# Two PSUM copies on ScalarE and eight token differences on GpSimd in a hybrid convolution and RWKV-7 step

## The chip, the cores and the metric

The kernel runs on one core of a Trainium2 chip. A core has a matrix engine (TensorE, PE in the profile, with its weight loads as PEld), a vector engine (VectorE, DVE), a scalar engine (ScalarE, ACT), a general engine (GpSimd, POOL), a queue engine that only issues transfers (SyncE, SP), and DMA engines. Each engine works through its own queue of instructions in order, and semaphores hold an instruction until what it needs is there. The metric is the device time of one execution in microseconds; 2640.5 us is the median of three runs before the change (2638.36 to 2641.32).

## What is computed

One inference step of a two-layer decoder over 1040 prompt positions (16 learned ones and 1024 tokens) and 8 separate single tokens. Layer 0 is a Conformer convolution and an MLP, layer 1 is an RWKV-7 time mixing and an MLP. The change concerns layer 1's mixer:

```python
def _wkv7_step(S, inp):
    r_t, w_t, k_t, v_t, kk_t, a_t = inp
    sa = jnp.einsum('bhvk,bhk->bhv', S, -kk_t)
    S = (S * w_t[:, :, None, :] + sa[..., None] * (kk_t * a_t)[:, :, None, :]
         + v_t[..., None] * k_t[:, :, None, :])
    y = jnp.einsum('bhvk,bhk->bhv', S, r_t)
    return S, y

def _rwkv7(h, shift_prev, S0, x_mix, w_r, w_k, w_v, w_o, ...):
    prev = jnp.concatenate([shift_prev[:, None, :].astype(h.dtype), h[:, :-1]], axis=1)
    xx = prev - h
    xr = h + xx * x_mix[0]
    ...
    r = (xr @ w_r).astype(f32)
    ...
    S_final, ys = lax.scan(_wkv7_step, S0.astype(f32), xs)
    ...
```

`xx` is the difference of each token's normalised row from the row before it. Every projection of the mixer reads a mixture `h + xx * x_mix[i]`. The scan updates one 64 x 64 state for each of 16 heads.

## The kernel before

Feature rows are kept transposed: 1024 features lie as KT = 8 blocks of 128 partitions, tokens run along the free dimension. Layer 0 goes through the tokens in three groups (352, 348, 348), the mixer in four (272, 256, 256, 264), layer 1's output projection and MLP again in three. The MLPs split each operand into a rounded high part and a remainder: for every weight tile, ScalarE writes the high part (`load_w`, L158) and GpSimd the remainder in four subtractions of 256 columns (L165), and TensorE multiplies three times (L190 to L192). Five buffers hold the split weight tiles.

The mixer's differences are made in `prepare`. It loads `hx` (the normalised rows with the row before the group), and then for each of the eight blocks makes `xx` at L893, by GpSimd for blocks 2 and 5 and by VectorE for the other six. The mixture `mix` (L887, tile mx) reads `xx`. For the first group `prepare(0)` is called while layer 0's MLP still works on its last token group; each difference is placed with `issue_after` behind a remainder `hl` (L142) of that MLP, block k behind the remainder number k + 5. In that MLP, VectorE also rescales (L347) and adds the products to the residual h (L360), which frees the PSUM banks that TensorE's `out` products fill.

The recurrence runs in 17 chunks of 64 tokens (the first holds the 16 learned positions). Each chunk turns the scan into small matrix products over 16 heads. `front(c)` forms A (L1287) and moves its parts to SBUF by ScalarE (no, L1292) and VectorE (xa, L1295; nr, L1297). `chunk(c)` then forms gg, the transposes bT (L1356), W (L1363), copied by VectorE as w1 (L1365), po, and U (L1379), which is a triangular solve applied to W. U fills one PSUM bank: 128 partitions by 8 blocks by 64. Partitions 0 to 63 hold the first head of each pair and 64 to 127 the second. L1380 copies the lower half by VectorE into `uv[HALF[0], :, 0, :]`, L1381 the upper half by ScalarE into `uv[HALF[1], :, 1, :]`. The state product S (L1390) and the output product Y (L1399) read `uv`. fs and sv (L1405, L1408) on VectorE make the next state.

The banks for A, W, U, S, Y, and the transposes yn (L1559) of finished chunks, come from one PSUM pool of three ("w"); a tile that asks for a bank waits until the readers of its last owner are done.

The chunks are woven into the projections: generators yield waits, and `tick` and `advance` decide after which projection a chunk's next step is emitted. TensorE's order is that of the program (`manual_schedule` for the tensor engine around the mixer and layer 1's MLP). The queues of VectorE, ScalarE and GpSimd are written there by a planner that simulates the program with estimated durations; instructions marked `kept_place` hold their place in the program's order. So on these three engines the order of instructions is a result of the planner's estimates.

Of the kernel before, what the change touches and what calls it, by code (L numbers as in the profile page):

```python
# [43 lines left out]
HALF = [slice(0, HS), slice(HS, P)]  # L44


def hybrid_step(tc, x_prompt, x_sample, state_conv, state_shift, state_wkv, meta_tokens,
# [8 lines left out]
    nc = tc.nc  # L56
    ctx = ExitStack()
    with ctx:
# [57 lines left out]
        def vec(name, i):  # L116
            c = col[name] + i
            return pvec[:, c:c + 1]
# [75 lines left out]
        def bank(name, tag="mm"):  # L194
            return cur[tag].tile([P, 512], F32, name=name, tag=tag)
# [672 lines left out]
        def prepare(g):  # L868

            c0, n = G1[g]  # L870
            npr = min(c0 + n, NP_TOK) - c0
            nm = lambda s, *a: f"{s}{g}" + "".join(f"_{x}" for x in a)

            hx = hnp.tile([P, KT, 1 + N1], F32, name=nm("hx"), tag="hx")
            if g == 0:
                nc.gpsimd.memset(hx[:, :, 0:1], 0.0)
                nc.sync.dma_start(hx[:, :, 1:1 + n], d_hn[:, :, :n])
            else:
                nc.sync.dma_start(hx[:, :, :1 + n], d_hn[:, :, c0 - 1:c0 + n])
            yield  # L880
            xx = hnp.tile([P, KT, N1], F32, name=nm("xx"), tag="xx")

            def mix(i, k):

                t = mixp.tile([P, N1], F32, name=nm("mx", i, k), tag="mx")
                with nullcontext() if g else tc.issue_after(marks["out2"][2 * (k - KT) + 1 if i == 2 else -1]):
                    nc.vector.scalar_tensor_tensor(t[:, :n], xx[:, k, :n], vec("x_mix", i * KT + k), hx[:, k, 1:1 + n],  # L887
                                                   op0=ALU.mult, op1=ALU.add)
                return t[:, :n]
            act = []  # L890
            for k in range(KT):
                with tc.issue_after(decayed[g - 1] if g else marks["hl2"][k + 5]):
                    (nc.gpsimd if k % 3 == 2 else nc.vector).tensor_sub(xx[:, k, :npr], hx[:, k, 0:npr], hx[:, k, 1:1 + npr])  # L893
                    if npr < n:
                        nc.vector.tensor_sub(xx[:, k, npr:n], sps[:, k], hx[:, k, 1 + npr:1 + n])
                if g:
                    act.append(mix(2, k))
                yield
            prep[g] = mix, hx, act
# [67 lines left out]
        def mixer_in(g, tick):  # L967
# [148 lines left out]
            for p in range(KT):  # L1116
# [81 lines left out]
                if g < 3:  # L1198
                    if p == 0:
                        coming = ranked(PP, prepare(g + 1))  # L1200
                        next(coming)
                    if p == 1:
                        for _ in coming:
                            pass
                        ks = carry["keys"] = keys(g + 1, both)
                        next(ks)
                    for _ in keys_behind(p):
                        next(ks, None)
# [53 lines left out]
        kv = lambda t: t.rearrange("p (k v) -> p k v", k=KT)  # L1262
# [60 lines left out]
        def chunk(c):  # L1323
# [3 lines left out]
            sv, uv = st["sv"], st["uv"]  # L1327
# [6 lines left out]
            def quads(name, pairs, lhs, rhs):  # L1334
                ps = bank(f"{name}{c}", "w")
                for p in range(KT):
                    for i, o in pairs:
                        nc.tensor.matmul(ps[Q[o], p * 32:(p + 1) * 32], lhs(i, p), rhs(i, p), start=True, stop=True,
                                         tile_position=(32 * i, 32 * o))
                return ps, ps[:, :256].rearrange("p (k t) -> p k t", k=KT)  # L1340
            down, up = [(0, 1), (2, 3)], [(1, 0), (3, 2)]

            ps, _ = quads("gg", down, lambda i, p: no[Q[i], p, :], lambda i, p: x32[Q[i], p, :])
# [9 lines left out]
            for h in range(2):  # L1353
                ps = bank(f"bT{c}{h}", "w")
# [5 lines left out]
            ps = bank(f"W{c}", "w")  # L1360
# [15 lines left out]
            ps = bank(f"U{c}", "w")  # L1376
            for p in range(KT):
                for q in range(2):
                    nc.tensor.matmul(ps[HALF[q], p * HS:(p + 1) * HS], p64[HALF[q], p, :], w1[HALF[q], p, :], start=True, stop=True)  # L1379
            nc.vector.tensor_copy(uv[HALF[0], :, 0, :], kv(ps)[HALF[0]])  # L1380
            nc.scalar.copy(uv[HALF[1], :, 1, :], kv(ps)[HALF[1]])  # L1381
            yield RW[5]
            step(c + 1)
            yield RW[6]
# [2 lines left out]
            ps = bank(f"S{c}", "w")  # L1387
# [39 lines left out]
        def recurrence():  # L1427
            for c in range(NCH):
                yield from chunk(c)
# [174 lines left out]
        with in_order():  # L1604
            shift_in()
            for _ in prepare(0):
                pass
            carry["keys"] = keys(0, lambda: None)
            for _ in range(KT + 1):
                next(carry["keys"])  # L1610
            for g in range(4):
                mixer_in(g, lambda slow=1.0: tick(g, slow))
            for _ in range(4):
                tick(3, 1.0)
            carry["tail"]()
            invert()
            settle(-(-(sum(G2[0]) - META) // HS))
# [183 lines left out]
```

## Time and profile before

| | |
|---|---|
| median of three runs | 2640.5 us (2638.36 to 2641.32) |
| profiled execution | 2641.17 us, its span 2639.5 us |
| instructions | 51709 |
| mean granted TensorE clock | 0.993 |
| DMA | 400.24 MB, mean 152 GB/s |

The profile gives a busy time for each engine, the chain of work that ended last, groups of instructions by source line with mean duration and the idle time before them, and who waited for whom. A timeline row reads: start in us, us, engine, line, operation, output<-inputs, shapes, count, and in brackets the idle time of the engine before it with what ended that. A row with a count above one merges neighbours, and its time is that of all of them. A row of the view of stretches reads: from:to, length, the busy time of PE, PEld, DVE, ACT and POOL with their counts, the granted clock of TensorE, the DMA engines' share and GB/s. Layer 0 takes the time up to some 1060 us, the mixer from there to about 1705 us, with the last chunks of the recurrence woven into layer 1's output projection and MLP up to 1902 us.

### The profile page before, as it was taken

The page shows a single profiled execution, that of the slowest core. Times are in us where ns is not written, and L with a number is a line of the kernel's source. Part 1 is how long each engine was busy: PE and PEld are TensorE (multiplying, and loading weights), DVE is VectorE, ACT ScalarE, POOL GpSimd, SP SyncE. Part 2 cuts the span into 40 slices and gives each one's busy share as a digit, 9 for nine tenths or more (in the row PEclk, how much of TensorE's full clock was granted, in tenths as well). Part 3 has the DMA queues.
Part 4 walks back from the last instruction along what each step waited for, and adds up shares of the span by engine and source line. Part 5 has one row for each costly group of instructions (what it writes and reads, how often), then busy time and mean ns, then how long its engine had stood idle before and what let it go on. Part 6 is the DMA issues. An engine that isn't in the chain of part 4 may idle for free.

```text
span 2639.5 us, 51709 instructions
## 1 busy us (share of the span) xinstructions
PE 2584.5 (98%) x19956; PEld 2439.1 (92%) x19956; DVE 1720.5 (65%) x3610; ACT 1129.0 (43%) x2093; POOL 1453.0 (55%) x2060
## 2 busy tenths in 40 slices
PE   9999999999999999999999999999999999999998
PEld 8999999999999999877787877799999999999998
DVE  6999999997544444544867567686689544444435
ACT  5546435444534333233344545555444542222223
POOL 7677878878878777122111213476588763333331
PEclk9999999999999999999999999999999999999999
DMA  6663544554446543678876867898575542222211
GB/s 189 174 164 111 163 142 132 161 171 137 142 137 179 157 137 119 181 202 205 227 191 191 217 170 189 217 206 195 149 215 174 147 132 68 69 72 64 73 49 45
DMA packets 602060, 400.24 MB, mean 152 GB/s; under 512 B 96128, under 2 KB 548928, under 8 KB 601814
## 3 DMA queue, kind: packets, MB, share of 16 engines
q1 hardware_dynamic: 573764, 360.08, 49.7%
q0 software_dynamic: 8720, 26.35, 3.2%
q10 hardware_dynamic: 19330, 10.49, 1.4%
q8 instruction: 158, 2.59, 0.4%
q14 instruction: 88, 0.72, 0.1%
HBM read 338.94 MB, written 58.83 MB: 151 GB/s over the span
## 4 chain that ended last, share of the span: by engine, by line
PE 86%; DVE 8%; DMA 2%; ACT 2%; issue 1%; POOL 0%; ACTq 0%; SPq 0%; DVEq 0%; POOLq 0%
PE ps_in L190 8%; PE ps_in L192 8%; PE ps_in L191 8%; PE out L190 8%; PE out L191 8%; PE out L192 8%; PE pk L922 4%; PE pr L922 4%; PE pv L922 3%; PE ps_g L190 1%; PE ps_o L192 1%; PE ps_g L191 1%; PE ps_g L192 1%; PE ps_oo L190 1%; PE ps_o L190 1%
## 5 line engine op out<-in xcount | busy, mean ns | idle before, releaser
L165 POOL TENSOR_TENSOR wo_lo<-wo_raw,wo_hi 128x256 fp32r<-128x256 f32 x736 | 541.9, 769 | 286.2 <-ACT wo_hi L158 282.4
L165 POOL TENSOR_TENSOR wi_lo<-wi_raw,wi_hi 128x256 fp32r<-128x256 f32 x640 | 473.5, 772 | 241.7 <-ACT wi_hi L158 241.1
L190 PE MATMUL out<-hh,wo_hi 128*128 128x352 f32 (+2 forms) x1536 | 497.6, 324 | 10.5 <-DVE h L360 8.9
L360 DVE TENSOR_TENSOR h<-h,out 128x352 f32<-128x352 f32 (+2 forms) x768 | 386.7, 512 | 167.1 <-PE out L192 165.7
L190 PE MATMUL ps_in<-m_h,wi_hi 128*128 128x352 f32 (+2 forms) x1536 | 493.9, 322 | 0.0
L192 PE MATMUL ps_in<-m_l,wi_hi 128*128 128x352 f32 (+2 forms) x1536 | 492.7, 321 | 0.7 <-DVE m_l L288 0.7
L191 PE MATMUL out<-hh,wo_lo 128*128 128x352 f32 (+2 forms) x1536 | 492.5, 321 | 0.0
L191 PE MATMUL ps_in<-m_h,wi_lo 128*128 128x352 f32 (+2 forms) x1536 | 491.5, 320 | 0.0
L192 PE MATMUL out<-hl,wo_hi 128*128 128x352 f32 (+2 forms) x1536 | 490.8, 320 | 0.0
L542 DVE SCALAR_TENSOR_TENSOR cv<-u,wdw,cv 128x348 f32<-128x348 f32 (+2 forms) x720 | 378.9, 578 | 0.7
L158 ACT CAST wi_hi<-wi_raw 128x1024 fp32r<-128x1024 f32 x160 | 167.6, 1048 | 386.9 <-PE out L192 194.6
L158 ACT CAST wo_hi<-wo_raw 128x1024 fp32r<-128x1024 f32 x184 | 192.6, 1048 | 313.0 <-PE out L192 166.6
L190 PEld LDWEIGHTS out<-hh,wo_hi 128*128 128x128 f32 x1536 | 289.1, 188 | 16.4 <-DVE h L360 11.7
L190 PEld LDWEIGHTS ps_in<-m_h,wi_hi 128*128 128x128 f32 x1536 | 289.2, 188 | 1.5
L192 PEld LDWEIGHTS ps_in<-m_l,wi_hi 128*128 128x128 f32 x1536 | 288.2, 188 | 2.0 <-DVE m_l L288 1.5
L191 PEld LDWEIGHTS out<-hh,wo_lo 128*128 128x128 f32 x1536 | 288.5, 188 | 0.8
L191 PEld LDWEIGHTS ps_in<-m_h,wi_lo 128*128 128x128 f32 x1536 | 288.5, 188 | 0.6
L192 PEld LDWEIGHTS out<-hl,wo_hi 128*128 128x128 f32 x1536 | 288.2, 188 | 0.0
L347 DVE SCALAR_TENSOR_TENSOR ps_in<-ps_in,rs_m 128x352 f32<-128x352 f32 (+2 forms) x192 | 100.6, 525 | 256.1 <-PE ps_in L192 255.7
L142 DVE TENSOR_TENSOR hl<-ps_in,hh 128x352 fp32r<-128x352 f32 (+2 forms) x192 | 98.9, 515 | 124.0 <-ACT hh L141 123.9
L348 ACT ACTIVATE ps_in<-ps_in 128x352 f32<-128x352 f32 (+2 forms) x192 | 85.1, 444 | 129.5 <-DVE ps_in L347 129.3
L1099 POOL DMA_DIRECT2D d_n<-n x32 | 24.4, 762 | 189.1 <-DVE n L1089 97.6
(371 smaller groups left out, 4735.1 us busy)
## 6 DMA issues: line engine op xcount, KB each, us to landing
wi_raw<-in_w_mlp_in_dram SPq DMA_DIRECT2D x160, 512.0 KB
wo_raw<-in_w_mlp_out_dram SPq DMA_DIRECT2D x160, 512.0 KB
wk_raw<-in_rwkv_w_k_dram SPq DMA_DIRECT2D x32, 512.0 KB
wr_raw<-in_rwkv_w_r_dram SPq DMA_DIRECT2D x32, 512.0 KB
wv_raw<-in_rwkv_w_v_dram SPq DMA_DIRECT2D x32, 512.0 KB
d_ab<-ab POOLq DMA_DIRECT2D x32, 512.0 KB, 4.5
pg_raw<-in_conv_w_pw_dram SPq DMA_DIRECT2D x24, 512.0 KB
pa_raw<-in_conv_w_pw_dram SPq DMA_DIRECT2D x24, 512.0 KB
```

The source lines that it names most:

```text
L142: return eng_lo.tensor_sub(lo, src, hi.bitcast(F32))
L158: cast = nc.scalar.copy(hi[:, :a * b], raw[:, :a * b])
L165: eng_lo.tensor_sub(lo[:, cs], raw[:, cs], hi[:, cs].bitcast(F32))
L190: nc.tensor.matmul(ps, w[0], act[0], start=first, stop=False)
L191: nc.tensor.matmul(ps, w[1], act[0], start=False, stop=False)
L192: nc.tensor.matmul(ps, w[0], act[1], start=False, stop=last)
L347: nc.vector.scalar_tensor_tensor(s, s, 0.0, rs()[:, :n], op0=ALU.max, op1=ALU.mult)
L348: nc.scalar.activation(s, s, AF.Square)
L360: total = nc.vector.tensor_add(hv[:, 4 * i + m, :], hv[:, 4 * i + m, :], ps[:, :n])
L542: nc.vector.scalar_tensor_tensor(acc[m][:, :n], ug[:, m, j:j + n], wdw[:, m, j:j + 1], acc[m][:, :n], op0=ALU.mult, op1=ALU.add)
L922: nc.tensor.matmul(ps[:, :n], w[:, k, :], act[k], start=k == 0, stop=k == KT - 1)
L1099: nc.gpsimd.dma_start(d_n[ch0:ch0 + ncg, p].rearrange("c r t -> r c t"), n32[:, :ncg])
```

## The change

Two edits. In `prepare`, all eight differences of the first group go to GpSimd; the other three groups stay as they were. In `chunk`, both halves of U are copied by ScalarE, one after the other, in all 17 chunks.

```diff
                 with tc.issue_after(decayed[g - 1] if g else marks["hl2"][k + 5]):
-                    (nc.gpsimd if k % 3 == 2 else nc.vector).tensor_sub(xx[:, k, :npr], hx[:, k, 0:npr], hx[:, k, 1:1 + npr])
+                    (nc.gpsimd if k % 3 == 2 or not g else nc.vector).tensor_sub(xx[:, k, :npr], hx[:, k, 0:npr], hx[:, k, 1:1 + npr])
...
             for p in range(KT):
                 for q in range(2):
                     nc.tensor.matmul(ps[HALF[q], p * HS:(p + 1) * HS], p64[HALF[q], p, :], w1[HALF[q], p, :], start=True, stop=True)
-            nc.vector.tensor_copy(uv[HALF[0], :, 0, :], kv(ps)[HALF[0]])
-            nc.scalar.copy(uv[HALF[1], :, 1, :], kv(ps)[HALF[1]])
+            for q in range(2):
+                nc.scalar.copy(uv[HALF[q], :, q, :], kv(ps)[HALF[q]])
             yield RW[5]
```

## The prediction

> **What bounds the kernel now.** The first view is the page: the engines' shares and the chain of work that ended last.
>
> ```profile
> PE 2584.5 (98%) x19956; PEld 2439.1 (92%) x19956; DVE 1720.5 (65%) x3610; ACT 1129.0 (43%) x2093; POOL 1453.0 (55%) x2060
> ...
> PE 86%; DVE 8%; DMA 2%; ACT 2%; issue 1%; POOL 0%; ACTq 0%; SPq 0%; DVEq 0%; POOLq 0%
> ```
>
> TensorE (PE) sets the end, and the change touches none of its instructions. So the question is narrow: which of TensorE's waits does the change shorten or create? The second view is the list of who TensorE waited for (total us, times, longest).
>
> ```profile
> PE out L190 <- DVE h L360: 8.9, 8, 2.3
> PE bT L1356 <- DVE nr L1297: 4.5, 5, 3.3
> PE A L1287 <- DVE fs L1405: 3.6, 2, 2.6
> PE yn L1559 <- ACT uv L1381: 3.2, 1, 3.2
> PE gg L1338 <- ACT em L1159: 3.0, 1, 3.0
> PE Y L1397 <- DVE nr L1297: 2.6, 2, 1.6
> ```
>
> Two single waits stand out: the longest on h (2.3) and the one on uv (3.2). The change edits the neighbourhood of both. GpSimd (POOL) ends none of the long ones.
>
> **Part one: token differences of the first group.** The tile view of xx (ns, minimum/median/maximum; the mixing mx in the whole run, the differences up to 1060 us), then the timelines of the three engines:
>
> ```profile
> L887 DVE SCALAR_TENSOR_TENSOR mx<-xx,pvec,hx x128: 460/485/1291, 1062.9 to 1546.7; 128x256 f32<-128x256 f32 x64, 128x272 f32<-128x272 f32 x32, 128x264 f32<-128x264 f32 x32
> L893 DVE TENSOR_TENSOR xx<-hx x6: 434/505/5217, 863.1 to 921.8; 128x272 f32<-128x272 f32 x6
> L893 POOL TENSOR_TENSOR xx<-hx x2: 642/642/643, 855.6 to 856.2; 128x272 f32<-128x272 f32 x2
> 855.62 1.24 POOL L893 TENSOR_TENSOR xx<-hx 128x272 f32<-128x272 f32 x2 [3.29 <-DMA hx<-d_hn]
> 856.82 5.62 POOL L165 TENSOR_TENSOR wi_lo<-wi_raw,wi_hi 128x256 fp32r<-128x256 f32 x8
> 862.39 5.59 POOL L165 TENSOR_TENSOR wo_lo<-wo_raw,wo_hi 128x256 fp32r<-128x256 f32 x8
> 871.19 1.43 POOL L165 TENSOR_TENSOR wi_lo<-wi_raw,wi_hi 128x256 fp32r<-128x256 f32 x2 [3.21 <-ACT wi_hi L158]
> 863.06 5.22 DVE L893 TENSOR_TENSOR xx<-hx 128x272 f32<-128x272 f32 x1
> 868.20 0.93 DVE L360 TENSOR_TENSOR h<-h,out 128x348 f32<-128x348 f32 x2
> 868.76 0.43 PE L190 MATMUL out<-hh,wo_hi 128*128 128x348 f32 x1 [2.33 <-DVE h L360]
> ```
>
> One difference on VectorE (DVE) took 5.22 us where the shortest took 0.434. It began while GpSimd ran sixteen subtractions without a pause (856.82 to 862.39 + 5.59 = 867.98) and finished 0.3 us after them. Behind it stood the additions L360 that empty PSUM, and TensorE stood 2.33 us for them. The change takes all six differences away from VectorE, so nothing of this kind is left there. Gain: at most 2.33, since no wait gives back more than its length; at least 0, if another late link ends at the same place. I take 2.33, because the additions have no other work of VectorE ahead of them.
>
> What it adds: six differences on GpSimd, 6 x 0.642 = 3.85 us. If all stand where the two stand now, GpSimd's stream reaches its 871.19 work about 3.85 - 3.21 = 0.64 us late. What hides it: the first weight tile behind the differences is done halfway through the eight subtractions at 856.82, near 859.6, and TensorE first uses it at the row below, 10.3 us later. Without that cover it would be 3.85 us; with it, I count nothing.
>
> ```profile
> 869.98 0.32 PE L191 MATMUL ps_in<-m_h,wi_lo 128*128 128x348 f32 x1
> ```
>
> Queued behind the moved differences are only these weight tiles; no DMA moves. The wait for hx (3.29) stands at the head already. The mixing mx that reads xx starts at 1062.9, far from the last difference at 921.8.
>
> **Part two: the U copies, once in each of 17 chunks.** The tile view of U, with the waits that ended at its readers:
>
> ```profile
> L1380 DVE COPY uv<-U x17: 657/682/684, 1306.9 to 1897.1; 64x512 f32<-64x512 f32 x17
> L1381 ACT COPY uv<-U x17: 581/582/585, 1307.6 to 1897.8; 64x512 f32<-64x512 f32 x17
>   DVE uv L1380: 32.5, 14
>   PE U L1379: 5.4, 9
> ```
>
> The two halves do not run side by side today: ScalarE (ACT) stood 32.5 us in 14 chunks until VectorE's half was done. So two copies on ScalarE replace a chain of 0.682 + 0.582 = 1.26 by 2 x 0.582 = 1.16, with no handover and no place in VectorE's queue. ScalarE's busy time grows by 17 x 0.582 = 9.9 us, while 32.5 us of standing still go. The place where this reaches TensorE is chunk 3:
>
> ```profile
> 1436.14 1.15 PE L1379 MATMUL U<-w,p 64*64 64x64 f32 x32
> 1434.78 1.51 ACT L1535 ACTIVATE ez<-yn,pvec 128x128 f32<-128x128 f32 x4 [0.46 <-ACT vt L1072]
> 1441.74 0.68 DVE L1380 COPY uv<-U 64x512 f32<-64x512 f32 x1
> 1442.46 0.58 ACT L1381 COPY uv<-U 64x512 f32<-64x512 f32 x1 [6.17 <-DVE uv L1380]
> 1438.76 1.16 PE L1287 MATMUL A<-xa,bk 64*128 64x128 f32 x16
> 1443.09 0.66 PE L1559 MATMUL yn<-ident,ey 128*128 128x128 f32 x4 [3.17 <-ACT uv L1381]
> ```
>
> U ends at 1437.29 and ScalarE is free from 1436.29, but VectorE reaches its half at 1441.74. The transposes yn need the PSUM bank that U occupies, so TensorE stands 3.17 us. With both copies on ScalarE the bank is free at about 1437.3 + 1.2 = 1438.5, before A ends at 1439.92. Gain: between 0 and 3.17; I take 3.17. Late next are the PSUM readers of A on VectorE, whose queue gets 0.6 us shorter.
>
> Taking 0.68 from VectorE also shortens its queue elsewhere. That counts only where its work is unbroken from the copy to something TensorE waits for.
>
> ```profile
> 1569.60:1583.50 13.90, 9.79 (x169) 8.26 (x165) 13.32 (x37) 4.95 (x15) 3.00 (x6) 0.92 0.49 115
> 1599.50:1604.00 4.50, 3.61 (x50) 2.81 (x48) 4.45 (x13) 1.09 (x3) 1.97 (x5) 1.00 0.35 102
> 1599.50 0.68 DVE L1380 COPY uv<-U 64x512 f32<-64x512 f32 x1
> 1600.11 0.34 DVE L1350 TENSOR_SCALAR p<-p,par32q 128x256 f32<-128x256 f32 x1
> 1604.05 0.65 PE L1397 MATMUL Y<-sv,xa 128*64 128x64 f32 x15 [0.94 <-DVE nr L1297]
> 1583.54 0.69 PE L1356 MATMUL bT<-ident,bk 128*128 128x128 f32 x2 [3.31 <-DVE nr L1297]
> ```
>
> In the stretch rows (length, busy us of PE, PEld, DVE, ACT and POOL, then the granted clock) VectorE is busy 13.32 of 13.90 and 4.45 of 4.50, each from a copy to a wait on nr. The next instruction starts 1600.11 - 1599.50 = 0.61 later, so about 0.6 comes off each: 1.2 us. Bounds: 0, and 17 x 0.61 = 10.4 if every chunk passed it on.
>
> The cost: ScalarE's second copy delays what stands behind it, by up to 0.58, where ScalarE comes late by itself.
>
> ```profile
> 1570.49 0.58 ACT L1381 COPY uv<-U 64x512 f32<-64x512 f32 x1
> 1573.43 0.39 PE L1390 MATMUL S<-uv,bkt 128*64 128x64 f32 x5
> ```
>
> There the pair would end near 1571.65 and S reads it at 1573.43; the cover is 1.8 us. I count nothing; without cover it is at most 0.58 a chunk, 9.9 us over all 17.
>
> **The sum.** The profiled execution took 2641.17 us, its span being 2639.5. Minus 2.33, 3.17 and 1.2 gives 2634.5. The median of the three runs shown, 2640.5, lies 0.7 below that execution, so I forecast 2634. What the sum cannot price is order: the queues of ScalarE, VectorE and GpSimd are arranged by a planner from estimated times, and both parts change these times, so other instructions may swap places. The clock makes such a swap dearer than its wait:
>
> ```profile
> 1615.50 0.70 PE L1338 MATMUL gg<-x,no 32*32 32x32 f32 x19 [3.04 <-ACT em L1159]
> 1615.30:1622.10 6.80, 6.49 (x49) 5.48 (x50) 4.15 (x15) 2.56 (x8) 1.06 (x4) 0.50 0.51 116
> 1436.20:1444.60 8.40, 5.22 (x64) 4.36 (x64) 8.37 (x22) 1.19 (x4) 2.15 (x4) 1.00 0.26 75
> ```
>
> After the 3.04 us wait, TensorE ran 6.8 us at clock 0.50; half of its 6.49 busy us, 3.25, was lost on top: 6.3 in all. After the 3.17 us wait of chunk 3 the clock stayed at 1.00, so I count only that wait's own length. A swap is worth -6.3 to +6.3 by this row; I take 0 and keep both ends.
>
> The Trainium skill ("TensorE: Matmul & The Clock Gate", section "What's actually happening") says that the gate watches a free-running window of 4096 cycles, 3413 ns, and halves the clock after an idle one. The 6.8 us stretch is two such windows; that a wait slightly longer than 3.04 left the clock alone fits a window that does not start with the wait.
>
> **The rivals.** *Slower: ScalarE becomes late.* In the recurrence, ScalarE's tanh, exp and vv feed the scan and TensorE; it stood ahead of TensorE's waits on em (3.0, in the list). If the planner puts the pair of copies in front of such work, ScalarE stands at U with it behind. Two such places, in a kernel that keeps only part one: 2640.5 - 2.3 + 2 x 6.3 = 2651. It decides from 7.6 us of new waits, beyond one such place. For it: the planned order can move anywhere between 1300 and 1900 us. Against it: ScalarE already stands 32.5 us at these copies, and would wait there for U alone.
>
> *Part two passes on.* TensorE gets past yn and stops soon after at other work of VectorE, which is booked solid there: 8.37 of 8.40 us. Then part one remains: 2640.5 - 2.3 = 2638. Against it: the yn group needs nothing else of VectorE.
>
> *Relief throughout.* If nearly every chunk passes on 0.61: 2640.5 - 2.3 - 3.2 - 10.4 = 2625. Against it: waits on nr and fs together are 10.7 us in the list, at few places.
>
> *The clock.* Work that comes 2.3 to 5.5 us earlier meets the gate's windows elsewhere. One stretch of 6.8 us fewer or more is about 3.3: 2631 or 2637. The clock row above bears out that waits of equal length differ; which way it falls is open.
>
> *The change does not do what it says*: the eight differences are spread over later gaps of GpSimd. The gain is the same, since VectorE is clear of them either way; no separate time.
>
> **How the numbers follow.** Chances: forecast 0.36 (own range 2629 to 2638), ScalarE late 0.25, part two passed on 0.16, relief throughout 0.12, the clock 0.11. About 0.2%, 5.3 us, is what a measurement can tell from no change: faster means below 2635.2, slower above 2645.8. Faster: 0.28 of the forecast, 0.11 of the relief, 0.06 of the clock, 0.45. Slower: 0.24 of ScalarE late. The rest, 0.31, is the same. The range from 2623 to 2651 reaches the relief and half of the slower case.
>
> **What would show it.** Right: eight xx on GpSimd before 930 us, at about 0.64 each and none on VectorE; no 2.3 us wait of TensorE near 866; 34 uv copies on ScalarE at 0.58, waiting for U alone; no wait of yn near 1437; VectorE busy some 19 us less (17 x 0.68, and the six differences with the held one). Wrong: a new wait of TensorE on GpSimd's weight tiles near 870, on em, vv or no of ScalarE between 1300 and 1900, or more stretches at clock 0.50 than before.

## The result and the profile after

| | before | after |
|---|---|---|
| median, us | 2641.3 | 2637.85 |
| ratio of the times, 95% interval | | 0.9984 [0.9978, 0.9990] |
| profiled execution, its span, us | 2641.17, 2639.5 | 2637.09, 2635.4 |
| granted clock of that execution | 0.993 | 0.994 |

The changed kernel is 0.16% faster, 4.2 us. The median came out 3.9 us above the 2634 that was forecast. Two of the 22 executions after the change took 3618.78 and 6682.36 us; the median counts them, the ratio and all means of spans below leave them out. First the engines' shares after the change and, of the list of who TensorE waited for (total us, times, longest), the rows that bear on the change:

```profile
PE 2581.3 (98%) x19956; PEld 2436.7 (92%) x19956; DVE 1707.6 (65%) x3587; ACT 1139.1 (43%) x2110; POOL 1457.0 (55%) x2066
...
PE out L190 <- DVE h L360: 7.6, 7, 1.6
PE A L1287 <- DVE fs L1405: 4.4, 4, 2.4
PE bT L1356 <- DVE nr L1297: 4.3, 4, 3.3
PE Y L1397 <- DVE nr L1297: 3.6, 2, 2.0
PE gg L1338 <- DVE ni L1250: 2.3, 1, 2.3
PE ps_oo L192 <- DVE z_l L142: 1.3, 1, 1.3
```

The wait on uv is gone from the list, and so is the 2.3 us wait on h. In their place stand two more waits on fs, a longer sum on nr at Y, a longer wait on z_l (0.4 before), and a shorter one at gg. TensorE's 19,956 matmuls are in the same order as before, so the two traces can be laid side by side matmul by matmul. The tile views of xx and uv, and the timeline around chunk 3's U, then its later row on fs:

```profile
L893 POOL TENSOR_TENSOR xx<-hx x8: 641/642/650, 855.1 to 862.0; 128x272 f32<-128x272 f32 x8
L1381 ACT COPY uv<-U x34: 572/581/585, 1301.9 to 1892.6; 64x512 f32<-64x512 f32 x34
  PE U L1379: 12.7, 11
...
1432.76 1.15 PE L1379 MATMUL U<-w,p 64*64 64x64 f32 x32
1433.95 1.17 ACT L1381 COPY uv<-U 64x512 f32<-64x512 f32 x2 [1.06 <-PE U L1379]
1435.37 1.16 PE L1287 MATMUL A<-xa,bk 64*128 64x128 f32 x16
1436.46 0.66 PE L1559 MATMUL yn<-ident,ey 128*128 128x128 f32 x4
1449.76 0.67 DVE L1405 TENSOR_TENSOR fs<-S,wc 128x512 f32<-128x512 f32 x1
1450.48 1.16 PE L1287 MATMUL A<-xa,bk 64*128 64x128 f32 x14 [0.66 <-DVE fs L1405]
```

The row of before at the same place on fs has no wait:

```profile
1455.96 1.16 PE L1287 MATMUL A<-xa,bk 64*128 64x128 f32 x16
```

The change does what it says. ScalarE's pair begins 0.04 us after U ends (1433.91), is done at 1435.12, and yn follows A without a wait. But 14 us later TensorE, which no longer stood for VectorE at yn, stands 0.66 us at fs, which it did not do before. Aligned by index, from start to start, the traces show 3.25 us won at yn (the lead goes from 3.38 to 6.63 us) and 1.14 us of it lost at fs and in A behind it (to 5.49).

### The profile page after: what moved, and what is told of

Same layout as the page of the kernel before. It is cut to its first block, busy times and chain, and to the rows that moved or that the text cites. A ratio compares the mean times of both kernels' runs of the same rounds, so it can differ in the third digit from the quotient of the medians.

```text
span 2635.4 us, 51726 instructions
## 1 busy us (share of the span) xinstructions
PE 2581.3 (98%) x19956; PEld 2436.7 (92%) x19956; DVE 1707.6 (65%) x3587; ACT 1139.1 (43%) x2110; POOL 1457.0 (55%) x2066
## 4 chain that ended last, share of the span: by engine, by line
PE 84%; DVE 9%; DMA 2%; ACT 2%; issue 2%; POOL 1%; ACTq 0%; SPq 0%; DVEq 0%; POOLq 0%
PE ps_in L190 8%; PE ps_in L192 8%; PE ps_in L191 8%; PE out L190 8%; PE out L191 8%; PE out L192 8%; PE pk L922 4%; PE pr L922 4%; PE pv L922 3%; PE ps_o L192 1%; PE ps_o L190 1%; PE ps_o L191 1%; PE ps_g L190 1%; PE ps_g L191 1%; PE ps_g L192 1%
## 5 line engine op out<-in xcount | busy, mean ns | idle before, releaser
L190 PEld LDWEIGHTS out<-hh,wo_hi 128*128 128x128 f32 x1536 | 289.1, 188 | 15.0 <-DVE h L360 10.4
```

What stands on the lines that cost most here:

```text
L190: nc.tensor.matmul(ps, w[0], act[0], start=first, stop=False)
```

## The experiments

Every ratio is against the kernel before, timed beside it on the same chip. "Clock" is the granted clock of a run, averaged over the runs of a kernel; the kernel before has 0.9929 over 101 runs. A mean clock of 11 or 12 runs is uncertain by about 0.0006 either way (twice its standard error), that of c3c7 by 0.0011.

| kernel | ratio, 95% interval | mean span, us | clock |
|---|---|---|---|
| part one alone (p1_only) | 1.0003 [0.9995, 1.0012] | 2640.9 | 0.9929 |
| block 0's difference alone (k0_only) | 0.9999 [0.9991, 1.0008] | 2640.1 | 0.9927 |
| first group all on VectorE (first_dve) | 1.0006 [0.9997, 1.0015] | 2640.7 | 0.9926 |
| the kernel before, again (before_again) | 1.0003 [0.9995, 1.0012] | 2640.3 | 0.9928 |
| part two alone (p2_only) | 0.9983 [0.9974, 0.9993] | 2635.5 | 0.9947 |
| part two in chunk 3 alone (c3_only) | 0.9991 [0.9982, 1.0000] | 2636.8 | 0.9932 |
| part one, and chunk 3 (c3_p1) | 0.9992 [0.9983, 1.0001] | 2638.4 | 0.9928 |
| part two but chunk 3 (but_c3) | 1.0000 [0.9991, 1.0009] | 2640.0 | 0.9937 |
| part two in chunks 3 and 7 (c3c7) | 0.9991 [0.9982, 1.0001] | 2637.6 | 0.9935 |
| part two but chunk 7 (p2_but_c7) | 0.9987 [0.9978, 0.9996] | 2636.7 | 0.9940 |
| part two but chunk 5 (p2_but_c5) | 0.9981 [0.9973, 0.9990] | 2635.0 | 0.9945 |
| the kernel after, again (after_again) | 0.9984 [0.9975, 0.9993] | 2635.7 | 0.9948 |

### Which part carries it

Part one alone, then part two alone:

```diff
-                    (nc.gpsimd if k % 3 == 2 else nc.vector).tensor_sub(xx[:, k, :npr], hx[:, k, 0:npr], hx[:, k, 1:1 + npr])
+                    (nc.gpsimd if k % 3 == 2 or not g else nc.vector).tensor_sub(xx[:, k, :npr], hx[:, k, 0:npr], hx[:, k, 1:1 + npr])
```

> Only the first edit: all eight differences of the first group on GpSimd, the U copies as before. The instruction order of ScalarE and SyncE stays as before, TensorE's too. My theory (one difference on VectorE was held 4.8 us by GpSimd's unbroken stream, and TensorE stood 2.33 us behind it): TensorE's wait of 2.33 near 866 us is gone, every later instruction of TensorE comes 2.4 us earlier, and the whole is 2.4 us shorter: ratio 0.9991. Rival (the clock's windows decide): the waits of the recurrence meet the windows elsewhere and the end moves by 2.4 plus or minus 3.3 us. Rival (GpSimd pays): a new wait on a weight tile near 870, and the ratio is 1.000.

```diff
-            nc.vector.tensor_copy(uv[HALF[0], :, 0, :], kv(ps)[HALF[0]])
-            nc.scalar.copy(uv[HALF[1], :, 1, :], kv(ps)[HALF[1]])
+            for q in range(2):
+                nc.scalar.copy(uv[HALF[q], :, q, :], kv(ps)[HALF[q]])
```

> Only the second edit: both halves of U copied by ScalarE in all 17 chunks. My theory (TensorE gains 3.0 us in chunk 3, and swapped instructions of the queues and waits for VectorE take back about 1.5 to 2.5 by the end): 0.5 to 2 us shorter, ratio 0.9992 to 0.9998. Rival (the two parts are independent and the second is worth what is left of 4.1 after 2.4): 1.7 us shorter with the same waits at the chunk 5 and 7 outputs (2.0 and 1.6 us) as with both edits. Rival (the copies themselves cost ScalarE's users): longer than before, ratio above 1.000.

Part two alone has the whole gain; part one has none. Yet part one's trace seemed to confirm the forecast: at 868 us it wins 2.6 us, counted from start to start, on the first profile of before (its lead goes from 0.62 to 3.22 us). Moving only block 0's difference shows the same 2.6 us, and no gain either:

```diff
+                    (nc.gpsimd if k % 3 == 2 or g + k == 0 else nc.vector).tensor_sub(xx[:, k, :npr], hx[:, k, 0:npr], hx[:, k, 1:1 + npr])
```

> Of the first group's differences only block 0 moves from VectorE to GpSimd, which then has blocks 0, 2 and 5; VectorE keeps 1, 3, 4, 6 and 7. No other instruction changes its place. My theory (only the difference that meets GpSimd's unbroken stream is held; the others fall where GpSimd pauses): the whole gain of the first edit, 2.4 us, ratio 0.9991, and the five differences left on VectorE at 0.43 to 0.51 us. Rival (the next difference on VectorE meets the longer stream in its place): one of the five takes 2 us or more, TensorE waits again, and less than 1 us is gained.

That left a lead that was won and never arrived. Two kernels went after it: one with all eight differences of the first group on VectorE, and the kernel before itself.

```diff
+                    (nc.gpsimd if k % 3 == 2 and g else nc.vector).tensor_sub(xx[:, k, :npr], hx[:, k, 0:npr], hx[:, k, 1:1 + npr])
```

> Neither part; instead all eight xx of the first group stand on VectorE, so that GpSimd begins its unbroken stream after nothing of the group. My theory (the 5.22 us of block 0 is time in which GpSimd's back-to-back operations hold VectorE's two-source operation): the stream begins earlier, at hx's arrival less nothing, and VectorE's first xx is held again as long as that stream lies in its way, so a held xx of 3 to 6 us appears again on VectorE and TensorE's wait near 866 us stays at 2 us or more. Rival (it was GpSimd's own two differences that delayed it): all eight run at about 0.38 us each, the wait near 866 is under 0.5 us and the trace is 2.3 us ahead there. By the end of the trace either is worth under 1 us, ratio 0.9996 to 1.0005, as with part one alone.

> The kernel before itself, unchanged, profiled a second time. My theory: every wait of TensorE over 0.5 us comes back with the same place and length to 0.1 us, while the stretches at clock 0.50 move, because they start at other multiples of the same step; so the two traces drift apart by 1 to 4 us at those stretches and nowhere else, and the ratio is 1.0000 within 0.0008. Rival (the clock stretches belong to the program): the same stretches at the same places to 1 us, and the traces agree to 0.5 us all along; then what part one lost at 1440 us is the change's own doing.

The timelines of the second profile of before, around the place where the first one has the 5.22 us difference:

```profile
856.10 5.64 POOL L165 TENSOR_TENSOR wi_lo<-wi_raw,wi_hi 128x256 fp32r<-128x256 f32 x8
861.68 5.84 POOL L165 TENSOR_TENSOR wo_lo<-wo_raw,wo_hi 128x256 fp32r<-128x256 f32 x8
862.86 0.57 DVE L893 TENSOR_TENSOR xx<-hx 128x272 f32<-128x272 f32 x1
863.35 1.54 DVE L360 TENSOR_TENSOR h<-h,out 128x348 f32<-128x348 f32 x3
866.07 0.32 PE L190 MATMUL out<-hh,wo_hi 128*128 128x348 f32 x1
1441.47 0.66 PE L1559 MATMUL yn<-ident,ey 128*128 128x128 f32 x4 [3.17 <-ACT uv L1381]
```

The same program, with the same unbroken run of sixteen subtractions on GpSimd, took 0.57 us for the difference, and TensorE went on at 866.07 without a wait. The wait on yn came back to the hundredth. So the 5.22 us belongs to one execution and the 3.17 us to the program. Nine profiles have block 0's difference on VectorE. It took 5.22 us in the first one of before and 0.43 to 1.03 us in the other eight (with all eight differences on VectorE, 0.43 us, GpSimd's run has pauses there), and all eight win the same 2.6 us on that first profile at this place, with part one or without. My theory of part one falls: what it removes is an event that came once in nine profiles. The rival expectation for the kernel with all eight on VectorE (no wait, some 2.3 us ahead) came true, but not by its reason, since the unchanged kernel does the same.

The second profile of before also shows where leads go. It was 3.1 us ahead of the first at 1266 us and ended 2.4 us behind it. Part of this is at a decode step woven into layer 1. The rows of the first profile, then of the second:

```profile
1933.04 0.43 DVE L1485 TENSOR_TENSOR t<-Sdec,dq 128x256 f32<-128x256 f32 x1 [1.99 <-DMA dq<-d_dec]
1934.87 0.63 DVE L1487 TENSOR_TENSOR Sdec<-Sdec,dq 128x256 f32<-128x256 f32 x1
1937.98 0.43 PE L190 MATMUL out<-hh,wo_hi 128*128 128x328 f32 x1 [1.13 <-DVE h L360]
```

```profile
1932.42 1.01 DVE L1485 TENSOR_TENSOR t<-Sdec,dq 128x256 f32<-128x256 f32 x1 [2.06 <-DMA dq<-d_dec]
1934.82 0.86 DVE L1487 TENSOR_TENSOR Sdec<-Sdec,dq 128x256 f32<-128x256 f32 x1
1938.15 0.60 PE L190 MATMUL out<-hh,wo_hi 128*128 128x328 f32 x1 [1.99 <-DVE h L360]
...
1938.20:1941.60 3.40, 3.40 (x13) 3.40 (x14) 2.61 (x7) 1.05 (x1) 0.35 (x2) 0.50 0.50 74
```

VectorE began 0.62 us earlier, but two of its operations took 0.81 us more, and TensorE, 0.69 us ahead, waited 0.86 us longer; a half-clock stretch followed, which the first profile does not have there. My expectation that TensorE's long waits come back to 0.1 us, with the drift at the clock alone, was thus wrong: those at yn, Y, gg, bT and U do, those on vv, fs (2.60 and 4.16 us near 1715) and h move by up to 1.6 us.

### Chunk 3 and the other sixteen chunks

Part two in chunk 3 alone, first with part one and then without it, and after them in every chunk except 3:

```diff
-            nc.vector.tensor_copy(uv[HALF[0], :, 0, :], kv(ps)[HALF[0]])
+            (nc.scalar.copy if c == 3 else nc.vector.tensor_copy)(uv[HALF[0], :, 0, :], kv(ps)[HALF[0]])
```

> The first edit, and the second in chunk 3 alone; the other 16 chunks copy as before. ScalarE's order differs by the one copy only, VectorE's by a few neighbours. My theory (the gain sits in two places, and what was lost came from swapped neighbours in the queues of chunks 5 and 7): both waits gone, 2.4 + 3.0 us, less 0.9 where TensorE meets VectorE in chunk 4: 4.5 us shorter, ratio 0.9983, and the waits of TensorE for nr in chunks 5 and 7 stay at 1.6 and 0.9. Rival (TensorE being earlier by itself brings the waits, since VectorE sets the pace there): these waits grow as with the full change, to 2.0 and 1.6, and the whole is 2.5 us shorter. Rival (the relief of VectorE in the other 16 chunks carries the gain): hardly shorter than the first edit alone.

> Part two in chunk 3 alone, the difference on VectorE as before. My theory: the yn wait of 3.17 us near 1437 us goes, some 0.9 of it returns as a wait on fs near 1456, and nothing else of part two happens, so -2.2 us, ratio 0.9991; the vv wait at 1266 and the nr waits of chunks 5 and 7 stay as before. Rival (the gain of part two is ScalarE's and VectorE's new order in all chunks): chunk 3 alone is worth under 1 us, ratio over 0.9996. Rival (clock windows set the time): the yn wait goes and the end still lies within 1 us of before, because a stretch at clock 0.50 stands somewhere where before has none.

```diff
+            (nc.scalar.copy if c != 3 else nc.vector.tensor_copy)(uv[HALF[0], :, 0, :], kv(ps)[HALF[0]])
```

> Part two in every chunk except 3, the difference as before. My theory: the yn wait of chunk 3 stays at 3.2 us, the vv wait of 0.67 at 1266 goes, the nr waits of chunks 5 and 7 grow by 0.4 and 0.7: together +0.4 us, ratio 1.0002, so that chunk 3 is all of part two. Rival (relief of VectorE in the other sixteen chunks is worth as much as chunk 3): -2 us, ratio 0.9992, with smaller waits on fs, no or h after 1700 us. The two ratios, this one and that of chunk 3 alone, must add up to that of part two alone (-0.0017) if the chunks act independently.

In the traces these behave as expected: with chunk 3 the yn wait goes and 0.65 to 0.87 us comes at fs; without it yn keeps 3.16 us. By ratio chunk 3 is worth 0.0009 and 0.0008, close to its net 2.1 us in the traces, the rest 0.0000, and part two whole 0.0017. With intervals of 0.0009 to either side, a remainder of 0.0008 is no proof that the parts need each other. But one column of the table separates better than the times: the granted clock. It is 0.9926 to 0.9932 in the kernels without part two or with chunk 3 alone, and 0.9945 to 0.9948 in part two alone, without chunk 5, and in the changed kernel in both its measurements. What that is worth is read within one kernel; the table has the three values that both kernels have:

| granted clock of the run | before: runs, mean span us | after, both measurements: runs, mean span us |
|---|---|---|
| 0.993 | 42, 2639.58 | 2, 2639.25 |
| 0.994 | 19, 2638.41 | 8, 2636.65 |
| 0.995 | 5, 2635.56 | 14, 2635.91 |

A straight line through the 101 runs of before falls 1.93 us for each 0.001 of clock; one through the 31 of after falls 1.73. At 0.994 the two lines give 2637.94 and 2637.18. The mean spans differ by 2640.06 - 2635.73 = 4.3 us. Of this, 0.0019 of clock at 1.73 to 1.93 is some 3.5 us, and only about 0.8 us is left at equal clock, a difference uncertain by about as much. That is an analysis of runs, not an experiment on the clock. Held against the line of before at its own mean clock, every one of the eight measurements with chunk 3's edit lies below it, by 0.6 to 2.7 us, and the five without it lie between 0.4 below and 1.5 above. So chunk 3's edit is worth something at equal clock too, 1.5 us in the mean of the eight. The kernel with part two everywhere but in chunk 3 is the one 1.5 above: its clock is up by 0.0008 and its time is not shorter, which nothing here explains.

### Where the clock comes from: a theory that fell

After the change the waits in chunk 7 are cut differently. VectorE's timeline before, then VectorE's and TensorE's after:

```profile
1602.32 0.68 DVE L1187 TENSOR_TENSOR ab<-rk,ex 128x512 f32<-128x512 f32 x1
1603.47 0.42 DVE L1297 TENSOR_TENSOR nr<-A,m_ar 128x256 f32<-128x256 f32 x1
1604.44 0.41 DVE L1297 TENSOR_TENSOR nr<-A,m_ar 128x256 f32<-128x256 f32 x1
1604.78 0.67 DVE L1188 TENSOR_TENSOR ab<-wa,em 128x512 f32<-128x512 f32 x1
1614.93 0.42 DVE L1297 TENSOR_TENSOR nr<-A,m_ar 128x256 f32<-128x256 f32 x1
```

```profile
1598.92 0.69 DVE L1187 TENSOR_TENSOR ab<-rk,ex 128x512 f32<-128x512 f32 x1
1600.38 0.69 DVE L1188 TENSOR_TENSOR ab<-wa,em 128x512 f32<-128x512 f32 x1
1601.11 0.42 DVE L1297 TENSOR_TENSOR nr<-A,m_ar 128x256 f32<-128x256 f32 x1
1601.67 1.15 PE L1397 MATMUL Y<-sv,xa 128*64 128x64 f32 x32 [1.65 <-DVE nr L1297]
1611.86 0.42 DVE L1297 TENSOR_TENSOR nr<-A,m_ar 128x256 f32<-128x256 f32 x1
1612.43 0.78 PE L1338 MATMUL gg<-x,no 32*32 32x32 f32 x32 [2.35 <-DVE ni L1250]
```

The planner has put ab L1188 ahead of nr. Y waits 1.65 us where it waited 0.94; eleven us later gg waits 2.35 us where it waited 3.04. The sum is the same, since VectorE sets the time of gg either way: an nr, which empties a bank of A, ends 0.15 us ahead of gg in both profiles (1615.35 before, 1612.28 after). The half-clock stretch behind gg was 6.8 us long in both profiles of before and 3.4 us in both of after. So the theory was that the shorter wait at gg keeps the clock up, and that chunk 7's copy causes it.

```diff
+            (nc.scalar.copy if c in (3, 7) else nc.vector.tensor_copy)(uv[HALF[0], :, 0, :], kv(ps)[HALF[0]])
```

> Part two in chunks 3 and 7 alone. By the waits: yn 3.17 us gone, fs +0.93 at 1456, Y +0.72 at 1604, gg 3.04 to 2.34 us (-0.70) at 1615, so -2.2 us as with chunk 3 alone, ratio 0.9991. My theory now (what part two gains beyond chunk 3 is granted clock, and it comes from the gg wait being shorter than one clock window): the mean granted clock of the runs rises from 0.993 (before, and chunk 3 alone) to 0.9945 or more and the ratio is 0.9985. Rival (the gain beyond chunk 3 is only the spread of the measurement, or it comes from the other chunks): the clock stays at 0.993 and the ratio at 0.9991.

```diff
+            (nc.scalar.copy if c != 7 else nc.vector.tensor_copy)(uv[HALF[0], :, 0, :], kv(ps)[HALF[0]])
```

> Part two in every chunk but 7. The waits at 1604 and 1615 go back to 0.93 and 3.04 us, the rest is as with part two alone. My theory (clock, from the gg wait of chunk 7): the mean granted clock falls back to 0.9935 or less and the ratio to 0.9990, slower than part two whole (0.9983), although the sum of the waits is the same. Rival (relief or clock from the other chunks): clock 0.9947, ratio 0.9983 or lower.

```diff
+            (nc.scalar.copy if c != 5 else nc.vector.tensor_copy)(uv[HALF[0], :, 0, :], kv(ps)[HALF[0]])
```

> Part two in every chunk but 5. The Y wait at 1529 goes back from 1.96 to 1.63 us, because ScalarE's wa step stands ahead of em and ex again: -0.4 us against part two whole, ratio 0.9982, clock 0.9947 as there. Rival (chunk 5 takes part in the gain of clock): clock 0.9935, ratio 0.9990.

> The changed kernel unchanged, profiled a second time. The waits on yn (none), Y at 1525 and 1600 (1.96, 1.65), gg (2.34), bT (3.25) and U (1.95) come back to 0.05 us; those on vv, z, the fs after 1700 us and h move by up to 2 us, as they did between two profiles of the kernel before. Mean granted clock 0.9948, ratio 0.9984. Rival (the first measurement was lucky): clock 0.993 and ratio 0.9990 or above.

TensorE's row at gg with chunks 3 and 7 alone, and the row of stretches behind it; then the same place in part two alone:

```profile
1612.55 1.06 PE L1338 MATMUL gg<-x,no 32*32 32x32 f32 x32 [2.45 <-DVE nr L1297]
1612.30:1619.10 6.80, 6.44 (x49) 5.40 (x50) 3.93 (x14) 3.17 (x10) 2.29 (x4) 0.50 0.43 98
```

```profile
1610.00:1617.00 7.00, 5.99 (x101) 5.00 (x103) 4.80 (x14) 3.45 (x11) 2.28 (x6) 1.00 0.40 126
```

With chunks 3 and 7 the wait at gg is 2.45 us, nearly as short as the theory wants, and the clock is still 0.50 for 6.8 us behind it; the mean clock is 0.9935 and the ratio 0.9991, not to be told from chunk 3 alone. Nor does the length of the wait go with the stretch elsewhere: part one alone, block 0 alone and the kernel with all on VectorE wait 3.03 to 3.04 us at gg, and the stretch behind it is 3.4 us there, as in after. The theory fails. Without chunk 7 the gg wait is 2.68 us and not 3.04, so the edits of other chunks shorten it too; the clock, 0.9940, and the ratio, 0.9987, lie between. Without chunk 5 the Y wait at 1525 us is back at 1.63 us (1.96 in part two alone), clock and ratio stay, and it is not distinguishable from the changed kernel. The second measurement of the kernel after gave the first one's ratio and clock again, so the gain is no luck of one measurement.

What stays open: which chunks' edits raise the granted clock by 0.0019. Chunk 3 alone does not do it, and leaving out chunk 5 or chunk 7 does not undo it. Nor do the profiles show one place: half-clock stretches before 2600 us add up to 24 to 38 us in the eight profiles without the second edit in most chunks and to 17 to 27 us in the six with it, spread over several places. One of these is the stretch near 1937 us shown above: it stands in six of the eight and in none of the six.

## Why the prediction was right, and where it was not

The direction was right and the time 3.9 us too low. By the prediction's own bound, faster below 2635.2 us, the measured 2637.85 still counts as the same, though the interval of the ratio leaves 1 out; it lies at the upper edge of the forecast's own range, 2629 to 2638. Of the 3.9 us, 0.8 is the base: the median of before is 2641.3 us over 22 runs, not the 2640.5 of three. The working had three terms, and only one of them is in the result, at two thirds of its size.

**"I take 2.33, because the additions have no other work of VectorE ahead of them."** This term failed. The additions did stand behind the difference, as its rows say, and with the difference on GpSimd TensorE does not wait there. But the hold of 5.22 us was one execution's: in the other eight profiles with that instruction on VectorE it is at most 1.03 us. By time part one is 1.0003. By time the bounds given, 0 to 2.33, held; the choice of the upper end took a maximum (434/505/5217 in the group's own row) for a property of the kernel. GpSimd's extra work was rightly counted at nothing: its next row below stands where TensorE does not wait, and the 3.21 us of idle time that stood ahead of it before has been used up.

```profile
871.03 1.44 POOL L165 TENSOR_TENSOR wi_lo<-wi_raw,wi_hi 128x256 fp32r<-128x256 f32 x2
```

**"Gain: between 0 and 3.17; I take 3.17."** The mechanism was right: the wait is in every profile without the edit of chunk 3, at 3.16 to 3.18 us, and in none with it. The size was off by what came back: of 3.25 us won in the trace 1.14 at fs, so 2.1 net, and chunk 3 alone measures 0.0009 (2.4 us, with an interval that just reaches 0). The text had named VectorE's readers of A as late next, without a price; what came was fs, VectorE's reader of S.

**"About 0.6 comes off each: 1.2 us."** Wrong in both places. The wait on bT is 3.25 us in place of 3.31. The one at Y grew by 0.71, because the planner used the freed place for ab and not for nr, and gg gave it back. VectorE's instructions did become 19.3 us shorter in sum, as forecast (its busy time, in which overlaps count once, fell by 12.9), but VectorE works in the planner's order, and nothing put nr first.

**The clock, ±3.3 us, chance 0.11.** By the analysis of the runs this was the larger part of the result: about 3.5 us of the 4.3, in the favourable direction, though as a mean over runs and not as one stretch more or fewer at a known place. The sum had no term for it, so that the time came inside the forecast's own range was in good part luck. One such stretch shows how a wait of the same length can cost more. After the 3.16 us yn wait of part one alone:

```profile
1438.50:1445.30 6.80, 5.56 (x15) 4.61 (x16) 6.55 (x19) 1.86 (x5) 0.75 (x1) 0.50 0.64 188
```

In six profiles with this wait, the clock stayed at 1.00 behind it twice and fell to 0.50 four times (in part one alone, block 0 alone, all on VectorE, and all but chunk 3), each time with 1.7 to 2.8 us of the lead lost. That is where the lead of part one's trace went first: 2.7 us of it.

**The rivals.** ScalarE late did not happen: the pair waited for U alone almost everywhere (12.7 us in 11 places, and no wait of TensorE on uv). Its small relative is chunk 5, where ScalarE's later step L1172 makes Y wait 1.96 us instead of 1.63. The wait on em in the list spoke less for this rival than the text took it to: gg's wait is put down to em in three of the fourteen profiles and to nr or ni of VectorE in the other eleven. "Part two passes on" happened to a third of the gain, 1.14 of 3.25 us. Relief throughout was not seen: part two without chunk 3 has the ratio 1.0000, whose interval leaves at most 2.4 us of the 10.4.

**The sum.** 2641.17 - 2.33 - 3.17 - 1.2 gave 2634.5, and from the median of three 2634. With the net of the waits (part one 0, chunk 3 -2.1, chunk 5 +0.3, chunk 7 0) the same sum gives -1.8, which the equal-clock comparison of the two kernels puts at -0.8, and the clock supplies the rest.

## What to carry to other kernels

Before a long instruction or wait is priced, look whether it comes back in a second profile of the same kernel; a group's maximum ten times its median is a question, not a cost. A wait that recurs to the hundredth in every profile, with a cause in the order of the program, is worth its length less what the next engine behind gives back; ask for that price too. Where effects are near 0.1%, compare the granted clock of the runs as well as their times: it told kernels apart here whose intervals overlap.

## What the hardware showed unexpectedly

**A hold that one execution in nine had.** In the first profile of before, GpSimd's next subtraction starts 0.04 us after the held difference, which began at 863.06 and ends only after seven of them:

```profile
863.10 1.44 POOL L165 TENSOR_TENSOR wo_lo<-wo_raw,wo_hi 128x256 fp32r<-128x256 f32 x2
```

The same pair of engines in part two alone, and then with all eight differences on VectorE:

```profile
863.15 0.74 POOL L165 TENSOR_TENSOR wo_lo<-wo_raw,wo_hi 128x256 fp32r<-128x256 f32 x1
863.22 0.97 DVE L893 TENSOR_TENSOR xx<-hx 128x272 f32<-128x272 f32 x1
863.84 0.95 POOL L165 TENSOR_TENSOR wo_lo<-wo_raw,wo_hi 128x256 fp32r<-128x256 f32 x1
```

```profile
862.68 0.43 DVE L893 TENSOR_TENSOR xx<-hx 128x272 f32<-128x272 f32 x1
862.70 1.01 POOL L165 TENSOR_TENSOR wo_lo<-wo_raw,wo_hi 128x256 fp32r<-128x256 f32 x1
```

In the first the difference, begun during a subtraction of 0.74 us, lasted 0.97 us, and the next subtraction took 0.95 us. In the second, GpSimd started 0.02 us after the difference and took 1.01 us, while VectorE kept its 0.43. So either engine can be the one that waits. In the other six of these eight profiles, too, the next subtraction takes 0.94 to 0.95 us. The Trainium skill ("SBUF — State Buffer", section "SBUF: two separate sides") says that a VectorE operation with two SBUF inputs and a GpSimd operation that reads SBUF exclude each other, and that whichever starts first has the ports for its whole instruction. These two cases agree; the 5.22 us, seven instructions of GpSimd of which the first starts behind VectorE's record, does not follow from it, and why it came in this execution stays open. Not every long time is rare: an m_l of VectorE near 520 us, also beside an unbroken run of GpSimd, takes 3.10 to 3.14 us in each of the fourteen profiles.

**Half-clock stretches on a grid.** Within one profile they start at multiples of 3.413 us from each other (before: 1280.8, 1581.2 and 1615.3 us, 88 and 98 steps), and from profile to profile the grid moves. The Trainium skill ("TensorE: Matmul & The Clock Gate", section "What's actually happening") calls this a free-running window, and the traces agree. That would let the same program, with the same wait, lose the clock in one execution and keep it in the next; single profiles can't tell two kernels apart that differ by one such stretch.

The wait on yn shows how it may come about. Three rows, each one step of its profile's grid: part one alone just before its stretch, then the two steps of before that the wait falls on.

```profile
1435.09:1438.50 3.41, 1.50 (x18) 0.97 (x16) 3.41 (x9) 0.00 (x0) 0.91 (x3) 1.00 0.22 58
```

```profile
1437.85:1441.27 3.42, 2.07 (x21) 1.46 (x19) 3.42 (x10) 0.00 (x0) 1.40 (x3) 1.00 0.22 58
1441.27:1444.68 3.41, 1.59 (x9) 1.45 (x10) 3.36 (x9) 1.10 (x4) 0.75 (x1) 1.00 0.11 36
```

In the four profiles that lost the clock, TensorE is busy for 1.07 to 1.50 us of the step just before the stretch. In the two that kept it, both of before, the emptier of the two steps has 1.59 and 1.82 us. This is a tendency and not a shown rule: elsewhere a step with 1.54 us kept the clock (part one and chunk 3, at 1223.4 us), and one with 2.22 us lost it (chunks 3 and 7, at 1574.7 us).
